# S5 preparation moved from GpSimd to VectorE in small pieces over both MLPs, B without its zero blocks, the ReLU's square on ScalarE

## The chip, the cores and the metric

One NeuronCore of a Trainium2 chip runs the whole step in one launch. Its engines are named as the profile names them: PE (TensorE, matmuls), DVE (VectorE), ACT (ScalarE), POOL (GpSimd) and SP (SyncE, which issues most of the DMAs). The metric is device microseconds (us) of one execution, the median of the runs.

## The reference

One inference step of a four-layer decoder trunk, for 256 prompt tokens and 32 sample tokens together (288 columns). Layer i has the mixer i mod 3: spatial gating (SGU), RG-LRU, S5, and SGU again. After each mixer comes an MLP with a squared ReLU.

```python
def sqrelu_ffn(h, w1, w2):
    return jnp.square(jax.nn.relu(h @ w1)) @ w2

def s5_block(h, s_re, s_im, w_in, lam_re, lam_im, log_dt, b_re, b_im, c_re, c_im, d_skip, w_glu):
    u = h @ w_in
    dt = jnp.exp(log_dt.astype(f32))[:, None]
    mag = jnp.exp(lr * dt)
    ab_re, ab_im = mag * jnp.cos(li * dt), mag * jnp.sin(li * dt)
    zr, zi = ab_re - 1.0, ab_im
    den = lr * lr + li * li
    q_re = (zr * lr + zi * li) / den
    q_im = (zi * lr - zr * li) / den
    bb_re = q_re[..., None] * br - q_im[..., None] * bi
    bb_im = q_re[..., None] * bi + q_im[..., None] * br
    ...  # state recurrence with ab over the tokens, output through c, GELU, GLU

def trunk(x, conv0, h0, sre0, sim0, p, keep_chunk_v):
    for layer in range(DEPTH):
        h = rmsnorm(x, p['norm_mix'][layer])
        ...  # out = mixer(h) by kind = layer % 3
        x = x + out.astype(x.dtype)
        x = x + sqrelu_ffn(rmsnorm(x, p['norm_ffn'][layer]), p['w_ff1'][layer], p['w_ff2'][layer]).astype(x.dtype)
```

What matters here: everything in `s5_block` that does not depend on the tokens (the factors `ab`, `q`, the input matrices `bb`, powers of `ab` times C, tables of phases) can be worked out at any time before layer 2.

## The kernel before

Weights come in chunks of 1 MB: 12 for a mixer, 32 for an MLP, 44 a layer. A chunk c is loaded by SP into one of three `raw` buffers (L183), split by ACT into a high part `whi` (L206, two pieces) and by DVE into the low part `wlo` (L207, two pieces), and used by 48 matmuls of 288 columns in groups of three (`mm3`: L282 high x high, L283 high x low, L284 low x high). The split runs two chunks ahead. `raw` is free again when both pieces of `wlo` are made. In an MLP, FF1's result goes through ACT `Relu` (L396), DVE square (L402), ACT copy to `hh` (L278) and DVE subtraction to `hl` (L279).

The token-independent part of S5 is a list of background tasks. SGU0, the first mixer, takes the RG-LRU's parameters and the whole of `s5_params`. The first MLP (FFN0) and the second (FFN1) take the rest, one task at a time at 32 places each, with a lower priority (`PRI_SPARE`), so that a scheduler that orders each engine's instructions by priority and readiness fills the gaps with them. There are 8 blocks m of state dimensions, m 0 to 3 in FFN0 and 4 to 7 in FFN1. For a block, SP loads `bt`, `qb`, `cc`, `bs`; POOL makes the input matrix `bi` (L874 to L876) and the phase table `tab` (L929 to L931); DVE makes powers (L884, L888) and the turned B (L898, L899); PE multiplies these (`s5_kernels`, L912), ACT and DVE make `kt` from it (L917, L918); and SP stores `bi`, `tab`, `cn` and `kt` to DRAM (`scr`), from where layer 2 fetches them (`sci`, `sco`). The pool of tiles named bg is closed at an MLP's end, and the next mixer's tiles lie in the same memory, so its first writers wait until the last store out of it has landed.

Every engine executes its own instructions in order, SP its DMA issues too.

Of the kernel before, what the change touches and what calls it, by code (L numbers as in the profile page):

```python
# [75 lines left out]
def layout(inp):  # L76
# [43 lines left out]
    def state(v):  # L120
# [3 lines left out]
                           state(np.repeat(a['log_dt'][0][:, None], 64, 1))], axis=1)  # L124
    bt = np.zeros((P, 2, 32, P), f)
    bs = np.zeros((P, 2, 32, 32), f)
    cc = np.zeros((P, 2, 32, 16), f)
    for n in range(2):
        b = (a['b_re'], a['b_im'])[n][0].reshape(32, 2, 64, 16)
        c = (a['c_re'], a['c_im'])[n][0].reshape(32, 2, 16, 64)  # L130
        for g in range(2):
            for l in range(4):
                r = 32 * l + 16 * g
                bt[r:r + 16, n, :, 64 * g:64 * g + 64] = b[:, g].transpose(2, 0, 1)
            bs[64 * g:64 * g + 64, n, :, 16 * g:16 * g + 16] = b[:, g].transpose(1, 0, 2)
            cc[64 * g:64 * g + 64, n] = c[:, g].transpose(2, 0, 1)
# [86 lines left out]
def body(tc, a, o, layers=(0, 1, 2, 3)):  # L223
# [149 lines left out]
    background = []  # L373
    n_tasks = [0]

    def spare(upto=0):
        if len(background) > (upto or 0):
            with tc.high_priority(offset=-PRI_SPARE):
                background.pop(0)(state['bg'])

# [5 lines left out]
    def ffn(layer, gnext, upto):  # L386
        with tc.tile_pool(name=f"bg{layer}", bufs=1) as state['bg'], tc.tile_pool(name=f"ffn{layer}", bufs=1) as pool:
            hh, hl = shifted(pool, 'hh', 16, MOVE[layer][0]), shifted(pool, 'hl', 16, MOVE[layer][1])
            st = {}

            def before():
                st['r2'] = norm_factor(True)

            def evac1(m, ps):
                q = t_(tag='t')
                i = S.activation(q, ps[:, :T], AF.Relu)  # L396
                if not st.get('table'):
                    st['table'] = True
                    with tc.issue_after(i.ins):
                        S.activation(t_([P, 1], tag='one', bufs=1), eps, AF.Sqrt)  # L400
                q2 = t_(tag='t2')
                V.tensor_tensor(q2, q, q, op=OP.mult)  # L402
                split(hh[m], hl[m], q2)
                if m % 2:
                    spare(upto)

            for half in range(2):
# [4 lines left out]
                for m in range(KT):  # L412
# [17 lines left out]
                    spare(upto)  # L430
            while len(background) > (upto or 0):
                spare(upto)
# [307 lines left out]

    def s5_params(pool):
        n_ = [0]

# [27 lines left out]
        V.tensor_tensor(cs, k, k, op=OP.mult)  # L771
        V.tensor_scalar(cs, cs, -2.0, 1.0, op0=OP.mult, op1=OP.add)

        rc, rs = (v[:, 64:].rearrange('p (n i) -> p n i', n=6) for v in (cs, sn))
        fine, coarse = s5['fine'], s5['coarse']
        G.tensor_copy(fine[:, 0, :, 0], rc[:, 0])
        G.tensor_copy(fine[:, 1, :, 0], rs[:, 0])
        G.memset(coarse[:, 0, :, 0], 1.0)
        G.memset(coarse[:, 1, :, 0], 0.0)
        ta, tb = (pool.tile([P, 2, 32, 4], F32, name=f's5d{i}') for i in range(2))  # L780
        for tab, first in ((fine, 0), (coarse, 3)):
            for n in range(3):
# [49 lines left out]
    def s5_spread(pool):  # L832
        qq = s5['qq']
        for h in range(2):
            pt = sec()
            PE.transpose(pt[:, :P], qq[:, 2 * h:2 * h + 2].rearrange('p l i n -> p (l i n)'), ident)
            qs = pool.tile([P, P], F32, name=f'qs{h}')
            V.tensor_copy(qs, pt[:, :P])
            S.dma_start(s5['qd'][P * h:P * h + P], qs)

    def s5_loads(m):

        four = slice(4 * m, 4 * m + 4)
        bt, qb = bg_([P, 2, 4, P], 'bt', 2), bg_([P, 4, 2, P], 'qb', 2)
        cc, bs = bg_([P, 2, 4, 16], 'cc', 2), bg_([P, 2, 4, 32], 'bs', 2)
        qd = s5['qd']
        nc.sync.dma_start(qb.rearrange('p q n c -> p (q n c)'),
                          bass.AP(tensor=qd.tensor, offset=qd.offset + 8 * m * P, ap=[[64 * P, 4], [0, 32], [1, 8 * P]]))
        nc.sync.dma_start(bt, a['bt'][:, :, four])
        nc.sync.dma_start(cc, a['cc'][:, :, four])  # L850
        nc.sync.dma_start(bs, a['bs'][:, :, four])
        s5['in', m] = bt, qb, cc, bs

    def s5_store(m, what):

# [76 lines left out]

    def s5_begin(pool, m):
# [4 lines left out]
        s5_loads(m)  # L938

    if 2 in layers:  # L940
        HALF_M = KT // 2
        background += [s5_params, s5_spread]
        for m_ in range(KT):
            last = m_ % HALF_M == HALF_M - 1
            steps = [lambda p, m=m_: (s5_begin(p, m) if m % HALF_M == 0 else s5_store(m - 1, 'kt'), s5_inputs(m, 0, G)),
                     lambda p, m=m_: s5_powers(m, 0, V),
                     lambda p, m=m_, l=last: (s5_inputs(m, 1, G), l or s5_loads(m + 1)),
                     lambda p, m=m_: (s5_store(m, 'bi'), s5_powers(m, 1, V)),
                     lambda p, m=m_: (s5_store(m, 'cn'), s5_table(m, G)),
                     lambda p, m=m_: (s5_store(m, 'tab'), s5_turned(m, V)),  # L950
                     lambda p, m=m_: s5_kernels(m)]
            if last:
                steps.append(lambda p, m=m_: s5_store(m, 'kt'))
# [215 lines left out]
```

## Time and profile before

| | |
|---|---|
| median of three runs | 1302.77 us (1302.33 to 1305.66) |
| profiled execution | 1305.58 us, span 1303.5 us |
| PE busy | 1242.2 us, 95% of the span |
| DVE, ACT, POOL busy | 920.9, 619.8, 316.8 us |
| mean granted TensorE clock | 0.977 of full speed |
| MLPs: FFN0, FFN1, FFN2 | 215.40, 222.50, 197.70 us for the same 32 chunks |

Stretches are named by their times in us from the span's start: FFN0 117.3 to 332.7, RG-LRU 332.7 to 445.7, FFN1 445.7 to 668.2, S5 668.2 to 801.8, FFN2 801.8 to 999.5. A window's row gives its bounds, its length, the busy time (and count of instructions) of PE, PE's weight loads, DVE, ACT and POOL, then PEclk, the DMA share and GB/s. PEclk is the granted clock as a share of full speed (0.50 is 1.2 GHz, 1.00 is 2.4 GHz).

### The profile page before, as it was taken

Reading aid. Unit: us, or ns where it says so; the run is one execution under the profiler, and the core shown is the slowest. Engines: PE = TensorE matmul, PEld = TensorE weight load, DVE = VectorE, ACT = ScalarE, POOL = GpSimd, SP = SyncE. Lnnn points to the kernel's source line nnn. Section 1 sums busy time; section 2 is a strip of 40 time slices with the busy share of each in tenths; the row PEclk is TensorE's granted clock in tenths of the full one; section 3 lists DMA queues with packets and bytes.
Section 4 is the critical chain, followed back from the end, with each engine's and each line's share of the span. In section 5 each row is a group of like instructions: output and inputs, shape, how many; then the busy total and the mean of one; then the engine's idle time right before and its main releaser. Section 6 shows DMA issues by size and latency. Waiting matters only on the chain.

```text
span 1303.5 us, 23773 instructions
## 1 busy us (share of the span) xinstructions
PE 1242.2 (95%) x9802; PEld 1215.7 (93%) x9802; DVE 920.9 (71%) x1451; ACT 619.8 (48%) x1019; POOL 316.8 (24%) x356
## 2 busy tenths in 40 slices
PE   8998997999987987999999999999999999999997
PEld 7997996999977977999998899999999999999997
DVE  8899956877688998657777756655666677655653
ACT  5754422554475624345443345534544645534541
POOL 2239256002158776100111210000002231000010
PEclk9998999999988997999999999999999999999999
DMA  8525655755512657655548544554446334554431
GB/s 292 198 99 182 196 180 212 241 190 190 194 69 94 223 163 243 222 189 186 186 163 304 199 142 158 179 177 163 162 162 213 137 133 162 184 172 162 162 130 37
DMA packets 45373, 229.79 MB, mean 176 GB/s; under 512 B 6784, under 2 KB 10544, under 8 KB 22736
## 3 DMA queue, kind: packets, MB, share of 16 engines
q1 hardware_dynamic: 43552, 223.79, 50.1%
q0 software_dynamic: 848, 3.75, 0.8%
q8 instruction: 77, 1.26, 0.4%
q10 hardware_dynamic: 864, 0.72, 0.2%
q14 instruction: 32, 0.26, 0.1%
HBM read 213.65 MB, written 14.60 MB: 175 GB/s over the span
## 4 chain that ended last, share of the span: by engine, by line
PE 57%; DVE 8%; POOL 4%; ACT 2%; issue 1%; DMA 1%; DVEq 0%; SPq 0%; ACTq 0%; POOLq 0%
PE acc L282 18%; PE acc L284 18%; PE acc L283 18%; DVE wlo L207 2%; PE sec L1001 1%; DVE t L402 1%; DVE hl L279 1%; PE acc L1039 1%; ACT whi L206 1%; PE acc L1043 1%; POOL gyl L691 1%; POOL t L688 1%; DMA sci<-scr 1%; PE acc L993 0%; DVE ct L884 0%
## 5 line engine op out<-in xcount | busy, mean ns | idle before, releaser
L207 DVE TENSOR_TENSOR wlo<-raw,whi 128x1024 fp32r<-128x1024 f32 (+1 forms) x354 | 448.1, 1281 | 146.1 <-ACT whi L206 144.6
L206 ACT ACTIVATE whi<-raw 128x1024 fp32r<-128x1024 f32 (+1 forms) x354 | 363.9, 1048 | 361.8 <-PE acc L283 254.4
L282 PE MATMUL acc<-xh,whi 128*128 128x288 f32 x1472 | 442.6, 301 | 10.9 <-ACT whi L206 4.8
L284 PE MATMUL acc<-xh,wlo 128*128 128x288 f32 x1472 | 440.9, 300 | 11.1 <-DVE wlo L207 11.1
L283 PE MATMUL acc<-xl,whi 128*128 128x288 f32 x1472 | 435.6, 296 | 3.9 <-DVE xl L294 3.9
L282 PE MATMUL acc<-hh,whi 128*128 128x288 f32 x1024 | 304.9, 298 | 4.2 <-ACT hh L278 3.1
L283 PE MATMUL acc<-hl,whi 128*128 128x288 f32 x1024 | 304.0, 297 | 4.7 <-DVE hl L279 4.7
L284 PE MATMUL acc<-hh,wlo 128*128 128x288 f32 x1024 | 303.2, 296 | 2.1 <-DVE wlo L207 2.1
L282 PEld LDWEIGHTS acc<-xh,whi 128*128 128x128 f32 x1472 | 280.0, 190 | 14.2 <-ACT whi L206 5.4
L284 PEld LDWEIGHTS acc<-xh,wlo 128*128 128x128 f32 x1472 | 279.0, 190 | 14.9 <-DVE wlo L207 13.8
L283 PEld LDWEIGHTS acc<-xl,whi 128*128 128x128 f32 x1472 | 283.4, 193 | 6.2 <-DVE xl L294 5.1
L306 POOL TENSOR_TENSOR ss<-ss,sq 128x288 f32<-128x288 f32 x62 | 68.5, 1105 | 709.4 <-ACT sq L305 708.9
L283 PEld LDWEIGHTS acc<-hl,whi 128*128 128x128 f32 x1024 | 194.2, 190 | 5.9 <-DVE hl L279 5.7
L282 PEld LDWEIGHTS acc<-hh,whi 128*128 128x128 f32 x1024 | 194.2, 190 | 5.6 <-ACT hh L278 3.8
L284 PEld LDWEIGHTS acc<-hh,wlo 128*128 128x128 f32 x1024 | 194.5, 190 | 2.9 <-DVE wlo L207 2.5
L419 DVE TENSOR_TENSOR t<-acc,r 128x288 f32<-128x288 f32 x64 | 29.2, 457 | 137.8 <-PE acc L284 137.8
L278 ACT ACTIVATE hh<-t 128x288 fp32r<-128x288 f32 x128 | 56.9, 445 | 123.7 <-DVE t L402 123.7
L279 DVE TENSOR_TENSOR hl<-t,hh 128x288 fp32r<-128x288 f32 x128 | 66.2, 517 | 27.0 <-ACT hh L278 25.0
L402 DVE TENSOR_TENSOR t<-t 128x288 f32<-128x288 f32 x128 | 67.2, 525 | 4.6 <-ACT t L396 4.5
L396 ACT ACTIVATE t<-acc 128x288 f32<-128x288 f32 x128 | 51.1, 400 | 19.7 <-PE acc L284 17.8
L294 DVE SCALAR_TENSOR_TENSOR xl<-x,aux,xh 128x288 fp32r<-128x288 f32 x64 | 52.6, 827 | 7.1 <-ACT xh L293 7.1
L293 ACT ACTIVATE xh<-x,aux 128x288 fp32r<-128x288 f32 x64 | 33.6, 528 | 38.4 <-DVE x L526 20.7
(326 smaller groups left out, 1395.6 us busy)
## 6 DMA issues: line engine op xcount, KB each, us to landing
raw<-in_wall SPq DMA_DIRECT2D x173, 1024.0 KB, 4.9
sci<-scr SPq DMA_DIRECT2D x8, 768.0 KB, 7.5
sco<-scr SPq DMA_DIRECT2D x8, 768.0 KB, 9.3
bt<-in_bt SPq DMA_DIRECT2D x8, 512.0 KB, 9.9
scr<-cn SPq DMA_DIRECT2D x8, 512.0 KB, 3.0
qb<-qd SPq DMA_DIRECT2D x8, 512.0 KB
scr<-bi SPq DMA_DIRECT2D x8, 512.0 KB, 6.6
raw<-in_wall SPq DMA_DIRECT2D x4, 512.0 KB, 8.1
```

What stands on the lines that cost most here:

```text
L206: nc.scalar.activation(h[:, c], self.raw[i][:, c], AF.Copy)
L207: nc.vector.tensor_tensor(l[:, c], self.raw[i][:, c], h[:, c].bitcast(F32), op=OP.subtract)
L278: S.activation(h, src, AF.Copy)
L279: V.tensor_tensor(l, src, h.bitcast(F32), op=OP.subtract)
L282: PE.matmul(ps, wh, h, start=first, stop=False)
L283: PE.matmul(ps, wh, l, start=False, stop=False)
L284: PE.matmul(ps, wl, h, start=False, stop=last)
L293: S.activation(xh[k], x[k], AF.Copy, scale=A[g][:, k:k + 1])
L294: V.scalar_tensor_tensor(xl[k], x[k], A[g][:, k:k + 1], xh[k].bitcast(F32), op0=OP.mult, op1=OP.subtract)
L306: G.tensor_tensor(state['ss'], state['ss'], q, op=OP.add)
L396: i = S.activation(q, ps[:, :T], AF.Relu)
L402: V.tensor_tensor(q2, q, q, op=OP.mult)
```

## The change

- `s5_params` is cut into eight parts by `yield`; its small tables move from POOL to DVE; nothing of it is left in SGU0. FFN0 takes the eight parts, the begin, the spread and the blocks m 0 to 2 (`SIDE = 3`), FFN1 the blocks 3 to 7. The places share out the tasks evenly, with up to two at one place.
- All of `s5_inputs` and `s5_table` is on DVE. The layouts of `bt`, `qb` and `bi` have 64 columns where they had 128, half of them zeros; `bi` is stored by eight DMAs into a block of `scr` that two DMAs have filled with zeros.
- `qd` is written by four DMAs of SP where two of ACT wrote it.
- The ReLU's square is ACT's `Square` where it was DVE's product.

```diff
-    bt = np.zeros((P, 2, 32, P), f)
+    bt = np.zeros((P, 2, 32, 64), f)
...
+    def spare(upto=None):
+        if upto is not None:
+            n = -(-(len(background) - upto) // max(1, places[0])) if len(background) > upto else 0
+            places[0] -= 1
+            for _ in range(n):
+                with tc.high_priority(offset=-PRI_SPARE):
+                    background.pop(0)(state['bg'])
...
                 q2 = t_(tag='t2')
-                V.tensor_tensor(q2, q, q, op=OP.mult)
+                S.activation(q2, q, AF.Square)
                 split(hh[m], hl[m], q2)
...
-                spare(n_tasks[0])
+                if m == 0:
+                    places[0] = KT
+                spare(n_tasks[1] + n_tasks[2] if background else None)
...
         exp_(dt, ld, pool, 'dt')
         V.tensor_tensor(q, lr, dt, op=OP.mult)
+        yield
...
-            S.dma_start(s5['qd'][P * h:P * h + P], qs)
+            for g in range(2):
+                qd = s5['qd']
+                nc.sync.dma_start(bass.AP(tensor=qd.tensor, offset=qd.offset + 128 * P * h + 32 * P * g,
+                                          ap=[[64 * P, 2], [64, 64], [1, 64]]), qs[:, 64 * g:64 * g + 64])
...
         nc.sync.dma_start(bt, a['bt'][:, :, four])
+        for i in range(2):
+            nc.sync.dma_start(s5['scr'][m][:, 512 * i:512 * i + 512], s5['zero'])
...
-            nc.sync.dma_start(d[:, 0:1024], s5['bi'].rearrange('p n q c -> p (n q c)'))
+            v = d[:, 0:1024].rearrange('p (n q c) -> p n q c', n=2, q=4)
+            for i in range(8):
+                r = slice(16 * i, 16 * i + 16)
+                nc.sync.dma_start(v[r, :, :, 64 * (i % 2):64 * (i % 2) + 64], s5['bi'][r])
...
-            s5['bi'] = bg_([P, 2, 4, P], 'bi', 2)
+            s5['bi'] = bg_([P, 2, 4, 64], 'bi', 2)
...
-        background += [s5_params, s5_spread]
+        background += [part] * 8 + [lambda p: s5_begin(0), s5_spread]
+        n_tasks[0] = len(background)
         for m_ in range(KT):
...
+            steps += [lambda p, m=m_, n=new: (n or s5_store(m - 1, 'kt'), s5_inputs(m, 0, V)),
+                      lambda p, m=m_: (s5_inputs(m, 1, V), m + 1 not in (SIDE, KT) and s5_loads(m + 1)),
+                      lambda p, m=m_: (s5_store(m, 'bi'), s5_powers(m, 0, V)),
+                      lambda p, m=m_: s5_powers(m, 1, V),
+                      lambda p, m=m_: (s5_store(m, 'cn'), s5_table(m, V)),
+                      lambda p, m=m_: (s5_table2(m, V), s5_turned(m, V)),
+                      lambda p, m=m_: (s5_store(m, 'tab'), s5_kernels(m))]
             background += steps
+        background.append(lambda p: s5_store(KT - 1, 'kt'))
```

Three places of the order. PE, at the start of layer 2, before: the matmuls of the last block's kernels (L912) stand inside the second chunk of the layer, with some 33 matmuls of that chunk and the whole chunk's end still behind them, and then S5's first own matmuls (L993, on the token data `u`).

```order
L282 MATMUL acc_7433<-xh_95,whi_7337 128x288
L283 MATMUL acc_7433<-xl_103,whi_7337 128x288
L284 MATMUL acc_7433<-xh_95,wlo_7338 128x288
L912 MATMUL sec_7068<-cn_5027,bq_6995 32x128 x8
L282 MATMUL acc_7433<-xh_96,whi_7337 128x288
...
L284 MATMUL acc_7462<-xh_98,wlo_7338 128x288
L993 MATMUL acc_7497<-u_7489,ident 32x72 x16
L993 MATMUL acc_7550<-u_7491,ident 32x72 x16
```

The same place of the changed kernel (L933 is L912, L1029 is L993):

```order
L282 MATMUL acc_7540<-xh_98,whi_7414 128x288
L283 MATMUL acc_7540<-xl_106,whi_7414 128x288
L284 MATMUL acc_7540<-xh_98,wlo_7415 128x288
L933 MATMUL sec_7341<-cn_4994,bq_7267 32x128 x8
L1029 MATMUL acc_7575<-u_7567,ident 32x72 x16
L1029 MATMUL acc_7628<-u_7569,ident 32x72 x16
L282 MATMUL acc_7683<-xh_91,whi_7492 128x288
```

No chunk matmul is left between the kernels' matmuls and S5's first ones. At the start of RG-LRU the last block's kernels of FFN0 have moved in the same way, by half a chunk.

SP in FFN0, before: loads of chunks (`raw`) between the loads and stores of the S5 blocks.

```order
L183 DMA raw_2206<-in_wall 128x2048
L849 DMA bt_2336<-in_bt 128x2x512
L858 DMA scr_114<-bi_2201 128x1024
L183 DMA raw_2272<-in_wall 128x2048
L847 DMA qb_2839<-qd 128x1x1024
L849 DMA bt_2838<-in_bt 128x2x512
L183 DMA raw_2344<-in_wall 128x2048
L858 DMA scr_115<-bi_2685 128x1024
L858 DMA scr_116<-bi_3237 128x1024
L183 DMA raw_2411<-in_wall 128x2048
```

SP at the same work of the changed kernel (L879 is L858, L863 is L847):

```order
L863 DMA qb_2333<-qd 128x1x512
L183 DMA raw_2705<-in_wall 128x2048
L879 DMA scr_113<-bi_2263 16x8x64 x3
L183 DMA raw_2781<-in_wall 128x2048
L879 DMA scr_113<-bi_2263 16x8x64 x5
L183 DMA raw_2865<-in_wall 128x2048
L183 DMA raw_2949<-in_wall 128x2048
L863 DMA qb_2854<-qd 128x1x512
```

The eight stores of a block are dealt out in twos to fives between loads of chunks.

DVE at the start of FFN1, before: FF1's squares and the chunks' low parts, with powers of block 4.

```order
L207 TENSOR_TENSOR wlo_5017<-raw_4786,whi_5016 128x1024 x2
L402 TENSOR_TENSOR t_431_5012<-t_5008 128x288
L279 TENSOR_TENSOR hl<-t_431_5012,hh 128x288
L402 TENSOR_TENSOR t_433_5022<-t_5020 128x288
L207 TENSOR_TENSOR wlo_5104<-raw_4842,whi_5103 128x1024
```

DVE there in the changed kernel (L895 to L897 are `s5_inputs`, L905 and L909 powers, all of block 3):

```order
L207 TENSOR_TENSOR wlo_4984<-raw_4753,whi_4983 128x1024 x2
L895 TENSOR_TENSOR bi_5009<-bt_4999,qb_5000 128x256
L896 TENSOR_TENSOR bt_426_5010<-bt_4999,qb_5000 128x256
L895 TENSOR_TENSOR bi_5009<-bt_4999,qb_5000 128x256
L897 TENSOR_TENSOR bi_5009<-bi_5009,bt_426_5010 128x256
L905 TENSOR_TENSOR ct_438_5106<-cc_5001,s5pw 128x320
...
L279 TENSOR_TENSOR hl<-t_415_4979,hh 128x288
...
L207 TENSOR_TENSOR wlo_5075<-raw_4809,whi_5074 128x1024
```

Six instructions that read freshly loaded `bt` and `qb` stand ahead of the next `wlo` on DVE, where POOL did them before.

## Rows read from the trace of the kernel before

**Rows 1.** Windows by stage: SGU0's end, FFN0, FFN1, FFN2.
```profile
103.00:117.30 14.30, 8.28 (x54) 7.50 (x53) 14.30 (x40) 3.96 (x7) 11.76 (x20) 0.84 0.12 40
117.30:332.70 215.40, 206.76 (x1545) 203.84 (x1545) 158.16 (x227) 95.65 (x155) 69.70 (x55) 0.97 0.61 209
...
445.70:668.20 222.50, 209.29 (x1543) 205.34 (x1542) 170.90 (x226) 96.42 (x155) 71.59 (x54) 0.95 0.59 200
...
801.80:999.50 197.70, 197.70 (x1495) 197.59 (x1495) 120.59 (x166) 94.44 (x143) 7.30 (x6) 1.00 0.49 167
```

**Rows 2.** Waits of PE at SGU0's end, 103 to 117.3: total us, times, longest.
```profile
PE acc L282 <- ACT xh L293: 3.5, 1, 3.5
PE acc L283 <- DVE xl L294: 2.5, 2, 2.0
```

**Rows 3.** Waits of PE in FFN0.
```profile
PE acc L282 <- ACT whi L206: 5.9, 3, 4.8
PE acc L284 <- DVE wlo L207: 2.5, 3, 1.3
```

**Rows 4.** Waits of PE in FFN1.
```profile
PE acc L284 <- DVE wlo L207: 5.7, 5, 2.0
PE acc L283 <- DVE hl L279: 4.4, 2, 2.5
PE acc L282 <- ACT hh L278: 3.1, 2, 2.6
```

**Rows 5.** Windows behind three gaps of PE: SGU0's end, RG-LRU's start, RG-LRU's convolution.
```profile
112.80:119.60 6.80, 3.75 (x14) 3.44 (x15) 5.46 (x11) 3.10 (x7) 4.73 (x7) 0.50 0.57 213
...
349.00:354.00 5.00, 2.71 (x21) 2.51 (x20) 3.04 (x9) 0.00 (x0) 1.80 (x4) 1.00 0.69 233
375.60:382.40 6.80, 4.92 (x15) 4.04 (x16) 6.80 (x13) 3.44 (x6) 1.61 (x4) 0.50 0.00 0
```

**Rows 6.** Groups of DVE in FFN1: busy us, mean ns, idle before, releaser.
```profile
L207 DVE TENSOR_TENSOR wlo<-raw,whi 128x1024 fp32r<-128x1024 f32 x64 | 86.6, 1373 | 14.6 <-ACT whi L206 14.3
L402 DVE TENSOR_TENSOR t<-t 128x288 f32<-128x288 f32 x32 | 21.9, 686 | 0.3 <-ACT t L396 0.3
...
L884 DVE TENSOR_TENSOR ct<-cc,s5pw 128x320 f32<-128x320 f32 x16 | 10.5, 676 | 0.0
L888 DVE TENSOR_TENSOR cn<-ct,ct 64x320 f32<-64x320 f32 x16 | 9.8, 612 | 2.4 <-PE sec L912 2.3
```

**Rows 7.** Groups of DVE in FFN2.
```profile
L207 DVE TENSOR_TENSOR wlo<-raw,whi 128x1024 fp32r<-128x1024 f32 x62 | 74.5, 1222 | 27.1 <-ACT whi L206 26.7
L402 DVE TENSOR_TENSOR t<-t 128x288 f32<-128x288 f32 x32 | 14.5, 452 | 1.6 <-ACT t L396 1.6
```

**Rows 8.** Groups of DVE between 60 and 117.3, in and ahead of SGU0's end.
```profile
L761 DVE TENSOR_SCALAR s5w<-s5w 128x32 f32<-128x32 f32 x8 | 1.0, 176 | 0.0
...
L771 DVE TENSOR_TENSOR s5w<-s5w 128x256 f32<-128x256 f32 x1 | 0.4, 411 | 0.0
```

**Rows 9.** Group of ACT in FFN2: a square of 288 columns.
```profile
L305 ACT ACTIVATE sq<-x 128x288 f32<-128x288 f32 x6 | 2.6, 429 | 0.0
```

**Rows 10.** A wait of POOL from 117.3 to 668.2, on a block's loads.
```profile
POOL bi L874 <- DMA cc<-in_cc: 15.6, 1, 15.6
```

**Rows 11.** Timeline of SP in FFN0: start, length of the issues with their waits.
```profile
209.07 9.99 SPq L858 DMA_DIRECT2D scr<-bi  x2
```

**Rows 12.** Timelines of PE, SP, POOL at S5's start: start, length, idle before.
```profile
676.97 0.64 PE L912 MATMUL sec<-cn,bq 128*32 128x128 f32 x16
...
679.22 0.33 SPq L865 DMA_DIRECT2D scr<-kt  x1
...
681.45 0.19 POOL L1008 MEMSET X<- 128x8 f32 x3 [9.22 <-DMA scr<-kt]
...
682.30 0.97 PE L993 MATMUL acc<-u,ident 128*32 128x72 f32 x24
```

**Rows 13.** Timeline of PE at RG-LRU's start.
```profile
352.11 0.37 PE L282 MATMUL acc<-xh,whi 128*128 128x288 f32 x1 [2.29 <-DVE E L612]
```

More of the change, by code (lines that the diff above doesn't have):

```diff
@@ L133, in layout @@
                 r = 32 * l + 16 * g
-                bt[r:r + 16, n, :, 64 * g:64 * g + 64] = b[:, g].transpose(2, 0, 1)
+                bt[r:r + 16, n] = b[:, g].transpose(2, 0, 1)
             bs[64 * g:64 * g + 64, n, :, 16 * g:16 * g + 16] = b[:, g].transpose(1, 0, 2)
@@ L373, in body @@
     background = []
[L374 to L379, printed above, removed]
+    n_tasks, places = [0], [0]
+    def spare(upto=None):
[5 more added lines that the diff above has]
+                    background.pop(0)(state['bg'])
     def bg_(shape, tag, bufs=1, dt=F32):
@@ L389, in ffn @@
             st = {}
+            places[0] = 4 * KT
             def before():
@@ L430, in ffn @@
                     spare(upto)
-            while len(background) > (upto or 0):
-                spare(upto)
+            assert upto is None or len(background) <= upto
     def sgu(layer):
@@ L757, in s5_params @@
         V.tensor_tensor(th, li, dt, op=OP.mult)
+        yield
         an, k, sn, cs = w_(256), w_(256), w_(256), w_(256)
@@ L772, in s5_params @@
         V.tensor_scalar(cs, cs, -2.0, 1.0, op0=OP.mult, op1=OP.add)
+        yield
         rc, rs = (v[:, 64:].rearrange('p (n i) -> p n i', n=6) for v in (cs, sn))
         fine, coarse = s5['fine'], s5['coarse']
-        G.tensor_copy(fine[:, 0, :, 0], rc[:, 0])
-        G.tensor_copy(fine[:, 1, :, 0], rs[:, 0])
+        V.tensor_copy(fine[:, 0, :, 0], rc[:, 0])
+        V.tensor_copy(fine[:, 1, :, 0], rs[:, 0])
         G.memset(coarse[:, 0, :, 0], 1.0)
@@ L784, in s5_params @@
                 for t, f in ((ta, rc), (tb, rs)):
-                    G.tensor_tensor(t[:, :, :, :w], tab[:, :, :, :w], f[:, first + n][:, None, :, None].to_broadcast([P, 2, 32, w]), op=OP.mult)
-                G.tensor_tensor(tab[:, 0, :, w:2 * w], ta[:, 0, :, :w], tb[:, 1, :, :w], op=OP.subtract)
-                G.tensor_tensor(tab[:, 1, :, w:2 * w], ta[:, 1, :, :w], tb[:, 0, :, :w], op=OP.add)
+                    V.tensor_tensor(t[:, :, :, :w], tab[:, :, :, :w], f[:, first + n][:, None, :, None].to_broadcast([P, 2, 32, w]), op=OP.mult)
+                V.tensor_tensor(tab[:, 0, :, w:2 * w], ta[:, 0, :, :w], tb[:, 1, :, :w], op=OP.subtract)
+                V.tensor_tensor(tab[:, 1, :, w:2 * w], ta[:, 1, :, :w], tb[:, 0, :, :w], op=OP.add)
+            yield
         pw = s5['pw']
@@ L808, in s5_params @@
             V.tensor_scalar(pw[:, n, 2], pw[:, n, 1], -1.0, None, op0=OP.mult)
+        yield
         zr, zi, den = w_(), pw[:, 1, 1], w_()
@@ L824, in s5_params @@
         V.tensor_tensor(qi, qi, den, op=OP.mult)
+        yield
         qq = s5['qq']
@@ L869, in s5_inputs @@
         if n == 0:
-            s5['bi'] = bg_([P, 2, 4, P], 'bi', 2)
+            s5['bi'] = bg_([P, 2, 4, 64], 'bi', 2)
         bt, qb, cc, bs = s5['in', m]
         bi = s5['bi']
-        t1 = bg_([P, 4, P], 'bt1')
+        t1 = bg_([P, 4, 64], 'bt1')
         eng.tensor_tensor(bi[:, n], bt[:, 0], qb[:, :, n], op=OP.mult)
@@ L920, in s5_table @@
     def s5_table(m, eng):
-        tab = s5['tab'] = bg_([P, 2, 4, NBL], 'tab')
-        ta, tb = (bg_([P, 2, 4, NBL], n) for n in ('ta', 'tb'))
+        ta, tb = s5['tab_'] = [bg_([P, 2, 4, NBL], n) for n in ('ta', 'tb')]
         four = slice(4 * m, 4 * m + 4)
@@ L929, in s5_table, with s5_table2, s5_begin @@
                 eng.tensor_tensor(t[:, c].rearrange('p q (i j) -> p q i j', j=8), fine, step, op=OP.mult)
+    def s5_table2(m, eng):
+        tab = s5['tab'] = bg_([P, 2, 4, NBL], 'tab')
+        ta, tb = s5['tab_']
         eng.tensor_tensor(tab[:, 0], ta[:, 0], tb[:, 1], op=OP.subtract)
         eng.tensor_tensor(tab[:, 1], ta[:, 1], tb[:, 0], op=OP.add)
-    def s5_begin(pool, m):
+    def s5_begin(m):
         s5['kt'], s5['cn'] = bg_([P, 4, P], 'kt'), bg_([P, 2, 5, 4, 32], 'cn')
@@ L937, in s5_begin, with part @@
         G.memset(s5['cn'], 0.0)
-        s5_loads(m)
+        s5['zero'] = bg_([P, 512], 'zero')
+        G.memset(s5['zero'], 0.0)
     if 2 in layers:
-        HALF_M = KT // 2
-        background += [s5_params, s5_spread]
-        for m_ in range(KT):
[L944 to L953, printed above, removed]
+        SIDE = 3
+        gen = []
+        def part(p):
+            if not gen:
+                gen.append(s5_params(p))
+            next(gen[0], None)
+        background += [part] * 8 + [lambda p: s5_begin(0), s5_spread]
+        n_tasks[0] = len(background)
+        for m_ in range(KT):
+            new = m_ in (0, SIDE)
+            if m_ == SIDE:
+                background.append(lambda p, m=m_: s5_store(m - 1, 'kt'))
+                n_tasks.append(len(background))
+            steps = [lambda p, m=m_, n=new: (m and s5_begin(m), s5_loads(m))] if new else []
+            steps += [lambda p, m=m_, n=new: (n or s5_store(m - 1, 'kt'), s5_inputs(m, 0, V)),
[5 more added lines that the diff above has]
+                      lambda p, m=m_: (s5_store(m, 'tab'), s5_kernels(m))]
             background += steps
-        n_tasks[0] = len(background) - 1
+        background.append(lambda p: s5_store(KT - 1, 'kt'))
+        n_tasks.append(len(background) - n_tasks[1])
     def s5_layer(layer):
@@ L1120, in body @@
             while background:
-                spare()
+                background.pop(0)(state['bg'])
     S.activation(t_([P, 1], tag='one', bufs=1), eps, AF.Sqrt)
@@ L1137, in body @@
         kinds[layer % 3](layer)
-        ffn(layer, f'norm_mix{layers[n + 1]}' if n + 1 < len(layers) else None, len(background) // 2 if layer == 0 else 0 if background else None)
+        ffn(layer, f'norm_mix{layers[n + 1]}' if n + 1 < len(layers) else None, n_tasks[2] if layer == 0 and background else 0 if background else None)
     r = last_factor()
```

4 lines of the change are left out of this document (2 added, 2 removed).

## The prediction

> **What bounds the kernel now.** I read the windows by stage first, because the same MLP occurs four times and only the first two carry S5's preparation [rows 1]. FFN2, which has none, is the yardstick: 197.70 us with PE busy throughout at full clock. FFN0 takes 215.40 and FFN1 222.50, with PE busy 206.76 and 209.29 at a clock of 0.97 and 0.95. Both have 48 matmuls more, three blocks' kernels of some 0.57 us each (a run's length of 0.64 less its overlap with the next matmul [rows 12]), 1.7 us in all. So FFN0 loses 215.40 - 197.70 - 1.7 = 16.0 and FFN1 23.1 us. At SGU0's end PE is busy 8.28 of 14.30 us, while DVE is busy all the time [rows 1].
>
> Next the waits of PE in those stretches. At SGU0's end it is idle 6.0 us for `xh` and `xl` [rows 2]: DVE, then doing `s5_params`, is late with x. In FFN0 the big wait is for `whi`, 5.9 us, then 2.5 for `wlo` [rows 3]; in FFN1 13.2 us for `wlo`, `hl`, `hh` [rows 4]. The first comes from SP: two stores of `bi` held SP from 209.07 for 9.99 us until POOL had made `bi` [rows 11], and the next `raw` stood behind them. The others come from DVE, whose two-input instructions are stretched while POOL reads too: `wlo` takes 1373 ns in FFN1 and 1222 in FFN2 [rows 6, 7], the square 686 against 452. What the waits don't account for is clock: behind SGU0's gaps there are 6.80 us at 0.50 [rows 5], which is the 1.2 GHz level, and in RG-LRU's convolution, where PE is busy 4.92 of 6.80 us, another 6.80. A gap of 2.29 [rows 13] left the clock at 1.00 in its window [rows 5].
>
> **The parts of the change.**
>
> *What is removed.* SGU0 loses the S5 parameters: 6.0 us of waits, and of the stretch at 0.50 the part up to 117.3, 4.5 us, of which half comes back, 2.2. The rest of that stretch is in FFN0's 16.0. With FFN1's 23.1 the most there is to win is 6.0 + 2.2 + 16.0 + 23.1 = 47.3 us. POOL's `bi` and tables vanish from both MLPs, and with them the stretching of DVE and the stores that wait for POOL.
>
> *What DVE takes over.* The yardstick has 120.59 us of DVE [rows 1]; the squares leave it, 14.5 [rows 7], so 106.1. Per block DVE has four powers products and four differences at the stretched 676 and 612 ns [rows 6], 5.2 us as an upper bound, some 2 us of turned B and `kt` (an estimate, seven instructions of 128 columns below the 0.41 of 256), and now six input and six table instructions of 256 columns at 0.41 [rows 8], 5.0. That is 12.2 a block: 36.6 for FFN0's three, 61 for FFN1's five. The parameters are, by the order, some 170 instructions, most of 32 columns at 176 ns [rows 8], 30 us, plus POOL's small tables, some 6. FFN0 comes to 106.1 + 36.6 + 36 = 179, FFN1 to 167, both under the 197.70 that PE needs. DVE is thus no lighter than now (158.16 and 170.90), but nothing stretches it. A place comes at every chunk, 197.7/32 = 6.2 us apart, of which 106.1/32 = 3.3 are DVE's own MLP work. A task of a block is 12.2/7 = 1.7 us: one makes 5.0, two 6.8 at the places that take two, which the two chunks of lead absorb.
>
> *The square on ACT.* 32 squares of 429 ns [rows 9] are 13.7 us an MLP on an engine busy 94.44 of 197.70 [rows 1]. It also takes one change of engine out of the chain to `hh`. FFN2 and FFN3 have PE busy throughout, so it gives them nothing; I cost it at 0. Its cover is `whi` two chunks ahead; without that, a `whi` behind a square would be 0.43 late.
>
> *SP.* Per block 17 DMAs replace 8. The order deals the eight small stores out between chunk loads. An issue alone takes 0.33 us [rows 12], so a run of five costs a `raw` 1.7 us. No row shows such stores; from below they cost 0, from above a hold like the 9.99 us of [rows 11] each. I take 0, since they are made by DVE, in order, well before. The Trainium skill, page "DMA: Bandwidth & Descriptors", section "Rules for kernel authors", says to coalesce small transfers and that below 64 KB one pays mostly overhead; it speaks against these stores of 32 KB each, and by it the sum would go to that of the small stores below. No run yet shows it here.
>
> *DVE waiting for loads.* `s5_inputs` reads `bt` and `qb`. POOL waited 15.6 us for such loads at FFN1's start [rows 10], with nothing queued behind it. On DVE, in order, `wlo` of the next chunk and `hl` stand behind it, and PE behind `wlo`. The split runs two chunks ahead, which is some 12 us of cover, minus what DVE has to do in it. From 0 to 15.6 us; I take 3 for both MLPs together, nearer the lower end, because the cover takes most.
>
> *The start of S5.* This is a new loss. In the order the kernels' matmuls of block 7 stand directly ahead of S5's first matmuls. These need `u`, which DVE may write only when the last `kt` store has left the memory that S5's pool reuses: POOL's first memset there waited 9.22 us for exactly that store [rows 12]. Before, the chain ran from 676.97 (L912) over the store at 679.22 to 682.30 (L993), 5.3 us, all under the rest of two chunks [rows 12]. Now nothing is left to cover it: PE stands idle about 5.3 us (4.7 without the matmuls themselves, up to 7 if a `whi` on ACT and a `wlo` on DVE, 1.22 [rows 7], are served first). By [rows 5] gaps of this size also bring 6.80 us at half clock, 3.4, of which 2.5 where PE is idle in part of it; I take 3. Together 8.3.
>
> *The start of RG-LRU.* The same store already costs 2.29 us there [rows 13]. The kernels stand half a chunk later, 3.1 us, so the gap becomes 5.4, long enough for the half clock, 3 more: 6.1.
>
> **Sum.** 1305.58 - 47.3 + 3 + 8.3 + 6.1 = 1275.7 for an execution like the profiled one. That one lies 2.8 above the median, so 1273 us.
>
> **Rivals.**
>
> *The starts are cheaper.* If the store lands sooner or its chain is hidden by other work, the 14.4 us given back shrink to nothing: 1258.5 with the 3 us kept. For it: a store's landing is only part of the chain. Against: PE's order has no other work at S5's start.
>
> *DVE stands for loads.* If the 15.6 us of [rows 10] come on DVE in FFN1 and again in FFN0, less what two chunks cover, some 9 us remain twice with a half clock of 3 beside one: 18 more, 1273 + 21 - 3 = 1291. For it: the six instructions stand ahead of `wlo` in the order. Against: the blocks after the first are loaded a whole block ahead.
>
> *Small stores hold SP.* It ends slower. One hold of 9.99 us [rows 11] made `raw` late and PE idle 4.8 [rows 3], and 3 of clock follow. If the eight small stores hold SP about 10 us per block, that is 8 x 7.8 = 62 us: 1335. It decides from a hold of about 8 us on, less than which the three raw buffers hide. It is what the Trainium skill's rule on small transfers, named above, would do here.
>
> *The change doesn't do what it says.* If not POOL's reading but the amount of DVE work makes `wlo` late, then FFN0 and FFN1 keep their losses, since DVE keeps its 179 and 167 us: 1305.58 - 8.2 + 14.4 = 1311.8, at the median 1309. For it: DVE's total does not fall. Against: rows of equal work are 12% (`wlo`) and 52% (square) longer where POOL works [rows 6, 7].
>
> **How the numbers follow.** Forecast 0.52, cheaper starts 0.14, DVE on loads 0.22, small stores 0.05, no effect 0.07. The forecast's own range, from the bounds of its terms (starts 10 to 17, loads 0 to 6), is 1266 to 1281. The range of 1258 to 1296 takes in cheaper starts and DVE on loads with some spread, and leaves out 0.12 to 0.18. Three per mille, 3.9 us, is about what a measurement tells from no change: faster below 1298.9, slower above 1306.7. Slower is 0.05 + 0.07 = 0.12; of DVE on loads 0.05 reach into the same band; faster is the rest, 0.83.
>
> **What would show it.** FFN0 and FFN1 within 5 us of 199.4 with PE waits of a few us; SGU0's end without a wait over 1 us; `wlo` near 1222 ns in both MLPs; FFN2 and FFN3 as before; a PE gap of about 5 us ahead of L1029 released through `u` by the `kt` store, and one of about 5 ahead of RG-LRU's first chunk behind E, with 0.50 behind both. Wrong would be: PE waits on `whi` behind `raw` (small stores), on `wlo` with DVE idle for a DMA (loads), on `wlo` with DVE full (no effect), or no gap at the two starts.

## The result and the profile after

The changed kernel takes 1269.17 us (1268.66 to 1271.23), the one before in the same comparison 1304.22: a ratio of 0.9735 with a 95% interval of 0.9715 to 0.9755. The forecast was 1273, in a range of 1258 to 1296. The profiled execution took 1268.66 us, its span is 1267.0, 36.5 less than before.

The windows by stage of the changed kernel (SGU0's end, FFN0, RG-LRU, FFN1, S5, FFN2; columns as in [rows 1]):

```profile
94.00:110.20 16.20, 16.20 (x125) 16.20 (x124) 12.73 (x26) 7.53 (x14) 6.18 (x8) 1.00 0.63 207
110.20:310.40 200.20, 199.26 (x1529) 198.21 (x1528) 153.23 (x350) 110.23 (x186) 7.90 (x6) 1.00 0.60 199
310.40:427.00 116.60, 99.68 (x673) 94.40 (x673) 92.14 (x126) 68.53 (x113) 65.94 (x92) 0.91 0.37 125
427.00:627.80 200.80, 200.80 (x1559) 199.26 (x1559) 155.04 (x270) 110.78 (x191) 9.35 (x7) 1.00 0.72 229
627.80:765.50 137.70, 130.43 (x1602) 124.89 (x1601) 93.86 (x155) 55.69 (x115) 21.83 (x49) 0.98 0.55 196
765.50:963.10 197.60, 197.60 (x1495) 197.50 (x1494) 109.76 (x134) 106.62 (x175) 7.32 (x6) 1.00 0.49 167
```

Against [rows 1], FFN0 is 15.2 us shorter and FFN1 21.7; in both PE is busy practically all the time at full clock, and PE's waits in them are 0.9 us for `hl` in FFN0 and none in FFN1:

```profile
PE acc L283 <- DVE hl L279: 0.9, 1, 0.9
```

FFN0 starts at 110.2 where it started at 117.3: SGU0's end gives 7.1, and PE has no gap left in it. FFN2 is unchanged, with 11 us less of DVE and 12 more of ACT. The two stages between grew. Their windows in the kernel before, which were not shown ahead, are RG-LRU and S5:

```profile
332.70:445.70 113.00, 98.92 (x673) 94.12 (x673) 90.13 (x126) 67.50 (x113) 65.20 (x92) 0.92 0.38 129
668.20:801.80 133.60, 130.13 (x1602) 123.92 (x1601) 93.67 (x155) 55.76 (x114) 21.31 (x49) 1.00 0.57 202
```

So RG-LRU gives back 3.6 us and S5 4.1. The sum is -7.1 - 15.2 + 3.6 - 21.7 + 4.1 = -36.3 of the 36.5.

DVE's groups in FFN1 after, which answer to [rows 6]:

```profile
L207 DVE TENSOR_TENSOR wlo<-raw,whi 128x1024 fp32r<-128x1024 f32 x64 | 77.7, 1241 | 14.2 <-ACT whi L206 13.7
...
L909 DVE TENSOR_TENSOR cn<-ct,ct 64x320 f32<-64x320 f32 x20 | 9.7, 483 | 2.1 <-PE sec L933 2.0
L905 DVE TENSOR_TENSOR ct<-cc,s5pw 128x320 f32<-128x320 f32 x20 | 9.4, 484 | 0.0
...
L895 DVE TENSOR_TENSOR bi<-bt,qb 128x256 f32<-128x256 f32 x10 | 4.2, 420 | 1.8 <-DMA qb<-qd 1.6 <-DMA bt<-in_bt 0.2
```

With POOL out of the way `wlo` is back at 1241 ns from 1373, the powers at 484 and 483 from 676 and 612. The last row holds the whole of DVE's waiting for the newly loaded inputs in FFN1: 1.8 us.

The start of RG-LRU after, in the timelines of PE and DVE, and the start of S5 in those of PE, SP and POOL:

```profile
326.69 0.64 PE L933 MATMUL sec<-cn,bq 128*32 128x128 f32 x16
333.72 0.58 PE L282 MATMUL acc<-xh,whi 128*128 128x288 f32 x1 [6.38 <-DVE E L618]
...
333.05 0.42 DVE L617 TENSOR_TENSOR E<-acc,r 128x256 f32<-128x256 f32 x1 [4.15 <-DMA scr<-kt]
...
640.88 0.65 PE L933 MATMUL sec<-cn,bq 128*32 128x128 f32 x16
646.50 2.29 PE L1029 MATMUL acc<-u,ident 128*32 128x72 f32 x64 [4.97 <-ACT dec L1041]
...
643.52 0.33 SPq L886 DMA_DIRECT2D scr<-kt  x1
...
645.83 0.19 POOL L1044 MEMSET X<- 128x8 f32 x3 [14.05 <-DMA scr<-kt]
...
645.94 1.55 DVE L1016 TENSOR_TENSOR u<-acc,r 128x288 f32<-128x288 f32 x4 [0.64 <-POOL X L1044]
```

Both gaps are there, 6.38 and 4.97 us. PE ends the last block's kernels, the `kt` copies, DVE's L939 and SP's store follow, and the first writers of the next mixer wait until the store has landed: DVE's E 4.15 us, POOL's X 14.05. At S5 DVE's `u`, which the first matmuls read, starts right behind POOL's X. The profile names PE's wait after `dec`, an ACT instruction that ended at about the same time (646.43) but that these matmuls do not read. The clock fell to half in both places:

```profile
329.80:336.60 6.80, 2.88 (x12) 2.91 (x13) 1.71 (x7) 0.53 (x1) 2.58 (x10) 0.51 0.51 158
...
643.90:650.70 6.80, 4.20 (x72) 4.01 (x73) 2.78 (x5) 1.69 (x5) 0.40 (x5) 0.50 0.74 270
```

### The profile page after: what moved, and what is told of

The parts are those of the page before. It is cut to its first block, busy times and chain, and to the rows that moved or that the text cites. A ratio compares the mean times of both kernels' runs of the same rounds, so it can differ in the third digit from the quotient of the medians.

```text
span 1267.0 us, 23878 instructions
## 1 busy us (share of the span) xinstructions
PE 1226.8 (97%) x9802; PEld 1205.5 (95%) x9802; DVE 862.7 (68%) x1445; ACT 671.9 (53%) x1148; POOL 181.8 (14%) x236
## 4 chain that ended last, share of the span: by engine, by line
PE 83%; DVE 8%; ACT 2%; DMA 2%; issue 2%; POOL 2%; SPq 0%; DVEq 0%; ACTq 0%; POOLq 0%
PE acc L284 26%; PE acc L282 26%; PE acc L283 26%; DVE wlo L207 2%; PE sec L1037 1%; ACT whi L206 1%; DVE xc L621 1%; DMA gb<-in_sgr 1%; DMA raw<-in_wall 1%; DMA sco<-scr 1%; PE acc L1079 1%; PE acc L1075 1%; DVE yl L279 1%; PE acc L1029 1%; DVE t L524 0%
## 5 line engine op out<-in xcount | busy, mean ns | idle before, releaser
L207 DVE TENSOR_TENSOR wlo<-raw,whi 128x1024 fp32r<-128x1024 f32 (+1 forms) x354 | 429.7, 1232 | 135.3 <-ACT whi L206 132.9
L279 DVE TENSOR_TENSOR hl<-t,hh 128x288 fp32r<-128x288 f32 x128 | 57.7, 451 | 34.3 <-ACT hh L278 34.3
L407 ACT ACTIVATE t<-t 128x288 f32<-128x288 f32 x128 | 56.0, 437 | 2.2 <-DVE hl L279 0.4
```

Source lines behind the costliest of these rows:

```text
L207: nc.vector.tensor_tensor(l[:, c], self.raw[i][:, c], h[:, c].bitcast(F32), op=OP.subtract)
L279: V.tensor_tensor(l, src, h.bitcast(F32), op=OP.subtract)
L407: S.activation(q2, q, AF.Square)
```

## The experiments

All ran beside the kernel before, and each ratio is to its median in the same comparison (1305.6 to 1306.37 us, where it was 1304.22 beside the changed kernel). Their medians are compared with 1269 us of the changed kernel. Windows and waits are from one profiled execution of each.

**One part taken back: the square on DVE.**

```diff
-                S.activation(q2, q, AF.Square)
+                V.tensor_tensor(q2, q, q, op=OP.mult)
```

> The changed kernel with the ReLU's square back on DVE. Theory (POOL's reads, not the amount of DVE work, made the MLPs slow): DVE gets 14.4 us more in each MLP, 168 and 169 of 200, nothing stretches it, and the time stays within 1268 to 1274 us; FFN2 and FFN3 stay at 197.6. Rival (the square on ACT is where the gain comes from): FFN0 and FFN1 lose a good part of their 15 and 22 us again, 1285 us or more.

Measured: 1272.34 us (1271.05 to 1274.1), ratio 0.9746 (0.9721 to 0.9772). Its FFN0 and FFN1:

```profile
110.10:310.30 200.20, 199.51 (x1529) 198.25 (x1528) 163.95 (x382) 96.81 (x154) 7.89 (x6) 1.00 0.60 199
428.00:630.60 202.60, 201.32 (x1559) 199.35 (x1558) 166.26 (x302) 97.26 (x159) 9.30 (x7) 1.00 0.72 227
```

DVE carries 11 us more in each, FFN0 does not notice, FFN1 is 1.8 longer. As the theory has it: with POOL quiet, the square's engine is worth some 2 us by the windows. The intervals of the two ratios, this one and that of the changed kernel, overlap, so the medians alone do not tell it from nothing.

**One part alone: the square on ACT in the kernel before.** The same line, the other way, in the kernel before.

> The kernel before with one part of the change alone: the ReLU's square on ACT. Theory (POOL's reads stretch DVE and hold SP): DVE loses the 16 and 22 us of stretched squares in FFN0 and FFN1, but the stores that hold SP and the stretch of the rest stay: a third of the loss at most comes back, 1290 to 1303 us. Rival (the square is where the change's gain comes from): 1285 or less.

Measured: 1295.72 us, ratio 0.9919 (0.9903 to 0.9935).

```profile
117.30:330.30 213.00, 205.06 (x1545) 203.06 (x1545) 148.27 (x195) 110.00 (x187) 72.09 (x55) 0.97 0.62 211
444.20:659.10 214.90, 205.53 (x1543) 203.22 (x1542) 156.59 (x195) 109.54 (x187) 72.35 (x54) 0.98 0.63 207
...
SPq L858 <- POOL bi L876: 30.2, 4, 13.1
...
PE acc L282 <- ACT whi L206: 7.4, 1, 7.4
...
L207 DVE TENSOR_TENSOR wlo<-raw,whi 128x1024 fp32r<-128x1024 f32 x64 | 88.2, 1406 | 25.1 <-ACT whi L206 24.8
```

FFN0 gets 2.4 us of its loss back and FFN1 7.6. SP is still held 30.2 us for POOL's `bi` in FFN0, PE still waits there for `whi` behind a late `raw` (7.4 us, 5.9 in [rows 3]), and `wlo` is as slow as before, at 1406 ns in FFN1. So taking work off DVE helps where POOL stretches it, but it cures neither cause.

**One part alone: inputs and tables on DVE in the kernel before,** zeros included, PE's order unchanged.

```diff
-  s5_inputs(m, 0, G)  s5_inputs(m, 1, G)  s5_table(m, G)
+  s5_inputs(m, 0, V)  s5_inputs(m, 1, V)  s5_table(m, V)
```

> The kernel before with one part of the change alone: its input matrices and phase tables on DVE at their full 128 columns, zeros included. PE's order is that of before to the instruction, so SGU0's end and the two starts stay. Theory (POOL's reads stretch DVE and hold SP): DVE gets 28 us more in each MLP and still the losses of 16 and 23 us shrink to 8 or less together: 1270 to 1285. Rival (the amount of DVE work is the bound): DVE comes to 185 of 200, the losses grow or stay: 1303 or more.

Measured: 1284.82 us (1280.79 to 1287.28), ratio 0.9834 (0.981 to 0.9858); its profiled execution took 1280.79, the low end of these, and has a span of 1279.1.

```profile
117.60:325.70 208.10, 205.43 (x1545) 203.69 (x1545) 161.05 (x275) 97.45 (x155) 10.83 (x7) 0.97 0.66 216
438.30:643.80 205.50, 202.06 (x1543) 200.43 (x1543) 162.35 (x274) 96.49 (x155) 8.03 (x7) 0.99 0.65 216
...
L207 DVE TENSOR_TENSOR wlo<-raw,whi 128x1024 fp32r<-128x1024 f32 x64 | 77.4, 1231 | 12.8 <-ACT whi L206 12.5
...
L874 DVE TENSOR_TENSOR bi<-bt,qb 128x512 f32<-128x512 f32 x8 | 5.5, 689 | 17.9 <-DMA scr<-bi 8.0 <-DMA qb<-qd 5.5 <-DMA bt<-in_bt 4.4
```

This is the clearest of them: DVE does all that POOL did, in the larger layout, and its busy time does not grow in FFN0 (161.05 after 158.16) and falls in FFN1 (162.35 after 170.90), because every two-input instruction is short again (`wlo` 1231 ns). FFN1 is 17 us shorter, FFN0 7.3. The rival of the prediction by which the amount of DVE work holds PE is out. The losses left, some 8.7 and 6 us counted as in the prediction, are more than the 8 together that the theory expected, though the median lies just inside its range. In FFN0 DVE itself now stands 17.9 us ahead of `bi` for a block's loads and for an earlier store of `bi` (the last row, of FFN0), which is the prediction's rival of DVE standing for loads; PE waits 2.6 us in all there, behind `hh` and `hl`, and the rest is PE's longer busy time at a clock of 0.97. The changed kernel has 1.4 and 0.8 us left: 200.2 and 200.8 less FFN2's 197.7 and less the blocks' kernels, of which two blocks lie in FFN0's window and four in FFN1's (1.1 and 2.3 us). Which of its other parts takes away the rest (half the columns, the tables in two tasks, the even spreading, the order of the loads, the parameters out of SGU0, the square) was not told apart.

The Trainium skill, page "SBUF — State Buffer", section "Who interferes with whom", says that VectorE's instructions with two inputs in SBUF contend with GpSimd's reads and those with at most one, outside VectorE's two-port modes, do not. The traces agree: in FFN1 L207 moved from 1373 to 1231 ns with POOL quiet; L419, with one of its two inputs in PSUM, stayed at 457 and 456, first before, then with the work on DVE:

```profile
L419 DVE TENSOR_TENSOR t<-acc,r 128x288 f32<-128x288 f32 x15 | 6.9, 457 | 26.3 <-PE acc L284 26.3
...
L419 DVE TENSOR_TENSOR t<-acc,r 128x288 f32<-128x288 f32 x15 | 6.8, 456 | 19.7 <-PE acc L284 19.7
```

**Back on POOL: inputs and tables of the changed kernel,** at half the columns.

```diff
-  s5_inputs(m, 0, V)  s5_inputs(m, 1, V)  s5_table(m, V)  s5_table2(m, V)
+  s5_inputs(m, 0, G)  s5_inputs(m, 1, G)  s5_table(m, G)  s5_table2(m, G)
```

> The changed kernel with the input matrices and phase tables back on POOL, at half the columns. Theory (POOL's reads stretch DVE): wlo, hl and cn in FFN0 and FFN1 grow from 1.22, 0.45 and 0.48 us again although DVE has less to do, stores of bi hold SP again, and PE waits come back: 1278 to 1292 us. Rival (the gain comes from the spreading of the tasks over the places and from what left SGU0): POOL has room, DVE gets 15 to 25 us lighter in each MLP, and the time stays at 1265 to 1272.

Measured: 1284.18 us (1283.68 to 1285.07), ratio 0.9837 (0.9812 to 0.9861). In FFN0, and in the last row in FFN1:

```profile
110.50:320.50 210.00, 202.23 (x1529) 200.48 (x1529) 154.10 (x315) 110.54 (x186) 46.33 (x42) 0.98 0.58 190
...
PE acc L283 <- DVE hl L279: 7.8, 3, 3.8
...
SPq L879 <- POOL bi L897: 8.4, 1, 8.4
...
L207 DVE TENSOR_TENSOR wlo<-raw,whi 128x1024 fp32r<-128x1024 f32 x64 | 83.5, 1333 | 18.9 <-ACT whi L206 18.6
```

FFN0 is 9.8 us longer though 35 instructions left DVE, whose busy time stays at 154; PE waits 7.8 us for `hl`, and SP is held 8.4 us for `bi` again, though no wait of PE for `whi` follows from it here. FFN1 is 3.7 longer, with `wlo` at 1333 ns after 1241; `cn` in FFN0, which the theory had listed too, stayed at 483 ns. The theory's range holds the time; the spreading alone, the rival, does not give it.

**The tasks end earlier:** 28 places where there were 32.

```diff
-            places[0] = 4 * KT
+            places[0] = 4 * KT - 4
```

> The changed kernel with the tasks of an MLP dealt out over its first 28 places, so that the last block's kernels stand at chunk 44.27 instead of 46.50 ahead of RG-LRU and at 88.35 instead of 90.00 ahead of S5. Theory (the last kt store holds the next mixer's first writers): the gaps of 6.38 and 4.97 us go to under 1 us each, and the two stretches at half clock behind them with them: 9 to 16 us less, 1253 to 1260. Rival (the norm's factor r, ready only some 5 us ahead of u, holds them): the gaps shrink by 0 to 2 us, 1266 to 1270.

Measured: 1255.17 us (1254.44 to 1256.47), ratio 0.9615 (0.9591 to 0.9639); once more, beside another kernel:

> The kernel with the early end once more, beside the one with the parameters in SGU0 on the same chip: 1253 to 1257 us by every theory; it is the yardstick for the other.

1255.76 us, ratio 0.962 (0.9601 to 0.964). RG-LRU and S5 in the first of these two comparisons, and PE at S5's start:

```profile
310.20:419.80 109.60, 97.18 (x674) 92.13 (x673) 91.18 (x126) 68.47 (x113) 64.31 (x92) 0.95 0.38 133
620.60:751.70 131.10, 129.25 (x1602) 123.85 (x1601) 94.09 (x155) 55.59 (x114) 22.22 (x49) 1.00 0.58 206
...
635.39 1.89 PE L1029 MATMUL acc<-u,ident 128*32 128x72 f32 x52 [0.80 <-ACT X L1045]
```

The gap at RG-LRU's start is gone, that at S5's is 0.80, and no stretch at half clock stands behind either. The stages are 7.0 and 6.6 us shorter than after the change, 13.6 of the 13.8 that separate the spans (1253.2 and 1267.0). The cause of the two new gaps is thus shown. This version is faster than both kernels.

**Earlier still:** 26 places.

> The changed kernel with the tasks dealt out over 26 places, which puts the last kernels at chunk 42.52 and 86.52. Theory (the gaps are gone once the store has landed ahead of the next mixer, and 28 places do that): no further gain, 1253 to 1257. Rival (the earlier the better, since the store chain still costs 0.8 us at S5's start and more elsewhere): 1252 or less. A denser DVE could also make it slower: over 1258.

Measured: 1255.59 us, ratio 0.9613 (0.9599 to 0.9628). No further gain, as the theory has it: once the store has landed in time there is nothing more to win. The rest of the gap at S5's start is still there, and POOL's X, made at 621.36, does not wait for the store any more, so the store is not its cause:

```profile
635.19 2.27 PE L1029 MATMUL acc<-u,ident 128*32 128x72 f32 x64 [0.70 <-PE acc L284]
```

**The parameters back in SGU0,** in their eight parts.

```diff
-                spare(n_tasks[1] + n_tasks[2] if background else None)
+                spare(n_tasks[1] + n_tasks[2] - 8 if background else None)
```

> The changed kernel with the eight parts of the S5 parameters taken by SGU0 again, one or two at a place. Theory (DVE at SGU0's end, full with the parameters, made xh and xl late): PE waits there for them again, 4 to 8 us with the clock, less than before's 8 since POOL does nothing in it; FFN0 gets back at most 1 us: 1272 to 1278. Rival (the small pieces alone cure it, wherever they are): no wait over 1 us there, 1266 to 1270.

Measured: 1264.89 us (1262.96 to 1265.74), ratio 0.9684 (0.9654 to 0.9713), below both expectations. SGU0's end has a wait, 2.2 us for `xl`, and starts FFN0 2.8 us later; but RG-LRU is short:

```profile
PE acc L283 <- DVE xl L294: 2.2, 2, 1.2
...
314.30:423.50 109.20, 98.42 (x658) 93.54 (x657) 90.65 (x125) 66.66 (x108) 63.37 (x92) 0.92 0.37 131
```

With fewer tasks in FFN0, one a place suffices, and the last kernels stand at chunk 41.54 instead of 46.50: the gap at RG-LRU's start is gone by the way, while that at S5's, 5.0 us, stays. To keep the two apart both edits were made together:

> The early end (28 places) together with the S5 parameters in SGU0. Theory (the parameters in SGU0 gained only because they let FFN0's last kernels end at chunk 41.54, which the early end gives anyway): SGU0's end and FFN0 are some 4 us slower, RG-LRU and S5 are those of the early end: 1257 to 1261 us. Rival (the parameters are better in SGU0 for a reason of their own): 1255 or less.

Measured: 1256.86 us (1256.04 to 1259.86) beside 1255.76 (1254.33 to 1256.14) without the parameters in SGU0. That is just under the theory's range and above the rival's. The gain is gone, so it was the earlier end; what the place of the parameters itself costs, 1.1 us between medians whose runs overlap, is not told from nothing. With the parts in SGU0 FFN0 starts 2.8 us later than without, and with the kernel before it started 7.1 later; so most of SGU0's loss before did not come from the place of `s5_params`. Whether it came from its being one task or from POOL's work in it was not told apart.

**One store for eight,** on the early end.

```diff
-            for i in range(8):
-                r = slice(16 * i, 16 * i + 16)
-                nc.sync.dma_start(v[r, :, :, 64 * (i % 2):64 * (i % 2) + 64], s5['bi'][r])
+            nc.sync.dma_start(d[:, 0:512], s5['bi'].rearrange('p n q c -> p (n q c)'))
```

> The kernel with the early end (28 places), and the eight small stores of a block's input matrix replaced by one contiguous store of the same bytes, so that layer 2 reads a wrong layout. Theory (the small stores cost nothing, as the sum took them): within 2 us of the kernel with the early end, 1253 to 1257. Rival (small transfers hold SP and the queue): 1245 or less.

Measured: 1261.11 us (1260.92 to 1263.92), ratio 0.9662 (0.9642 to 0.9683), slower than with the eight, which neither theory expected. FFN0 is what it was, FFN1 6.1 us longer than with the early end:

```profile
110.20:310.40 200.20, 199.27 (x1529) 198.21 (x1528) 153.22 (x350) 110.67 (x186) 7.85 (x6) 1.00 0.59 199
...
419.70:626.60 206.90, 202.53 (x1559) 200.75 (x1558) 154.47 (x269) 111.25 (x191) 9.21 (x7) 0.99 0.67 222
...
PE acc L283 <- DVE hl L279: 4.4, 1, 4.4
...
440.00:470.00 30.00, 30.00 (x229) 30.00 (x228) 27.29 (x65) 20.24 (x37) 0.00 (x0) 1.00 0.91 294
...
463.78 0.42 DVE L893 TENSOR_TENSOR bi<-bt,qb 128x256 f32<-128x256 f32 x1 [2.71 <-DMA bt<-in_bt]
```

With the early end the same 30 us of FFN1 are:

```profile
440.00:470.00 30.00, 30.00 (x229) 30.00 (x229) 24.59 (x49) 20.29 (x37) 0.00 (x0) 1.00 0.80 253
```

With seven issues a block fewer the order at FFN1's start came out otherwise: DVE does 65 instructions there instead of 49, it stands 2.71 us for a load ahead of `hl`, and PE waits 4.4 for that and loses the rest to a stretch at half clock behind it. That is the prediction's rival of DVE standing for loads, on a small scale; how much of it is the stand and how much the denser order was not told apart. In FFN0, where nothing else moved, eight stores or one make the same 200.20 us. The Trainium skill's rule on small transfers ("DMA: Bandwidth & Descriptors", section "Rules for kernel authors") thus shows no price in FFN0; in FFN1 the edit changed the order too, and what the stores cost there was not measured by itself.

## Why the prediction was right, point by point

- **What bounds FFN0 and FFN1** was read rightly: POOL's reads and the stores that wait for POOL. The windows of FFN0 and FFN1 are 15.2 and 21.7 us shorter, and with the kernels in them counted (one block fewer, one more) 14.6 of 16.0 and 22.3 of 23.1 us came back. Both single-part runs and the run back on POOL support it. How much of it is the stretching and how much the held stores was not measured apart, and inputs and tables on DVE alone leave 8.7 and 6 us, which went with the other parts of the change.
- **SGU0's end** was taken at 8.2 and gave 7.1.
- **DVE's load** was mis-sized, without effect on the time. The sum had 179 and 167 us, measured are 153.23 and 155.04. From FFN2's 109.76, a block is (155.04 - 109.76) / 5 = 9.1 us, not 12.2; 1.3 of the difference is that the powers were priced at their stretched length. The parameters are 153.23 - 109.76 - 3 x 9.1 = 16 us, not 36: the trace of FFN0 has 137 instructions of them and the spread, with durations that sum to 28 us. The rest of both differences is that the recorded durations of neighbours overlap, so that their sum is more than the busy time (see the last section).
- **DVE waiting for loads** was taken at 3; the row of L895 has 1.8 us in FFN1, FFN0 has none, and PE did not feel it.
- **The two starts** were right in mechanism and in the size of the gaps (5.3 at S5 and 5.4 at RG-LRU forecast, 4.97 and 6.38 measured), and too dear in the sum: 8.3 + 6.1 = 14.4 us were given back in the forecast, the stages grew by 4.1 and 3.6, 7.7 in all. Two things make the difference. The first is the term of the clock, 3 us each: PE is busy only 4.20 and 2.88 of the 6.80 us at half clock, the rest lies in the gap, and so the stretch costs at most half of that, 2.1 and 1.4. The second is that the stages gained elsewhere, which the sum did not have: with the early end, which has no gap but 0.80 us at S5, they take 131.1 and 109.6 us, 2.5 and 3.4 less than before. Of the 3.4 some 2.3 is the old gap at RG-LRU's start; the rest is not explained. Against the early end the two gaps with all that hangs on them cost 6.6 and 7.0 us, where the forecast's prices are 8.3 and, with the old gap of 2.29, 8.4. That PE's busy time in RG-LRU rose by only 0.76 (98.92 to 99.68) is no price of the new stretch, since the others in the stage became shorter: before there were 6.8 us in [rows 5] and these 10.3, after, these two beside the new one:

```profile
406.30:416.60 10.30, 7.10 (x28) 6.75 (x29) 5.77 (x8) 6.00 (x10) 9.38 (x14) 0.50 0.31 103
...
364.00:370.80 6.80, 4.84 (x11) 3.41 (x12) 5.98 (x8) 2.59 (x6) 1.95 (x2) 0.50 0.16 22
391.30:398.10 6.80, 5.13 (x20) 4.79 (x21) 5.93 (x8) 3.39 (x5) 5.88 (x7) 0.50 0.48 146
```

- **The square on ACT** was costed at 0 and is worth 1.8 us in FFN1 by the windows of the run without it; in the kernel before, with POOL at work, the same line was worth 10.
- **Small stores** were costed at 0. FFN0 agrees; FFN1 does not show them apart. The rival's figure of 8 us of hold that the three buffers hide does not fit its own rows: there a hold of 9.99 us left PE 4.8 idle, so some 5 were hidden.
- **The number** is nearer than its terms. For the profiled execution the forecast was 1275.7 and 1268.66 was measured: the starts were 6.7 too dear, the loads 3, and of the 47.3 to win 44.0 came (7.1 + 15.2 + 21.7). These errors go opposite ways. That the median, 1269.17, lies only 3.8 from the forecast of 1273 is in part luck: the forecast took 2.8 off for the step from the profiled execution to the median, and the changed kernel's profiled execution lies 0.5 below its median. Also, with the bounds given for its terms the forecast's own range around 1273 is 1266 to 1279; the 1281 was counted from 1275.7.

## What to carry to other kernels

When background work fills the gaps of a loop, look where its last store lands, not only where its work is done: memory that is handed to the next stage makes that stage's first writers wait, and four places earlier were worth 13.8 us of the span here. An engine that is "free" is not free if its work stretches the instructions of the engine on the path: `wlo` took 1373 ns with POOL at work and 1231 without, and moving POOL's work to the busier DVE shortened both MLPs. Price a stretch at half clock by PE's busy time in it, not by its length, since part of it lies in the gap. And price a gap against a run without it, as the early end is here: against the kernel before, other waits of the stage have moved too.

## What was not expected of the hardware

At S5's start PE was busy 4.20 of the 6.8 us at 0.50 of the clock, yet its busy time in the whole stage, with the same 1602 matmuls, is only 1.18 us above that with the early end (129.25), which has the stage at full clock, and 0.30 above that of before. Half of 4.20 would be 2.1; why it is less is not shown.

The recorded durations of short DVE instructions overlap. In a chain where each reads what the one before wrote, instructions of 32 columns start 0.22 us apart; where the next reads nothing of the one before, 0.10 us apart, though each is recorded with 0.17 to 0.19. FFN0 of the changed kernel, a pair of either kind:

```profile
112.11 0.18 DVE L555 TENSOR_SCALAR dt_p<-dt_p 128x32 f32<-128x32 f32 x1
112.33 0.19 DVE L558 TENSOR_TENSOR s5w<-dt_p,dt_i 128x32 f32<-128x32 f32 x1
...
132.08 0.17 DVE L808 TENSOR_TENSOR s5w<-s5pw 128x32 f32<-128x32 f32 x1
132.18 0.17 DVE L811 TENSOR_TENSOR s5w<-s5pw 128x32 f32<-128x32 f32 x1
```

So the parameters' instructions, whose durations sum to 28 us, added some 16 us to DVE's busy time.
